# Scale and shift of six feature tiles summed in PSUM by TensorE, with blocks of ada_w as weights

## The chip, the cores and the metric

The kernel runs on one core of a Trainium2 chip. The core has five engines that each take their own instructions in the order in which the program gives them: TensorE (PE; its weight loads are shown apart as PEld), VectorE (DVE), ScalarE (ACT), GpSimd (POOL) and SyncE (SP), whose queue issues most of the DMAs. The metric is the device time of one execution in microseconds. Three executions of the kernel before took 1699.92, 1700.15 and 1702.2 us.

## The reference, cut to what matters

One layer of a decoder trunk: a token-mixing part with four mixers, then an MLP, on 1024 tokens of 1024 features. The part in question is its first step: a normalised input, scaled and shifted per feature, which is then multiplied by the input projection.

```python
c_act = jax.nn.silu(c.astype(jnp.float32))                  # (1, 1024)
mod = (c_act @ ada_w[l] + ada_b[l])[:, None, :]             # (1, 1, 6144)
sh1, sc1, gt1, sh2, sc2, gt2 = jnp.split(mod, 6, axis=-1)
h = rms_norm(x, norm_mix_g[l]) * (1.0 + sc1) + sh1
p = h @ w_in[l]
```

`sh1` and `sc1` are the products of the 1024 values of `c_act` with the first 2048 columns of `ada_w`, which are 8 MB of float32. Every feature of h needs its own sum over 1024 rows of `ada_w`.

## The kernel before, in words

Features lie on partitions, tokens along the free axis. The 1024 features are eight tiles of 128 (`kt`, 0 to 7), the tokens two halves of 512. Each projection is done at float32 precision by three float32r matmuls: h is split into `hh` (rounded) and `hl` (the rest), the weights into `whi` and `wlo`, and `mm3` (L112) adds hh·whi, hl·whi and hh·wlo in PSUM. The text calls these 128x512 matmuls the wide ones.

The stage around the change is `start`. It takes the first three blocks of 128 columns of `w_in` (six PSUM banks, `pts`), loops over the feature tiles, and makes h on the way. For one feature tile `kt`:

- `ada_load` brings the columns of `ada_w` that give sh1 and sc1 of the tile (`ada`, two sections of 128 columns, all eight blocks of 128 rows). Tiles 0 and 1 are loaded alone, 2 and 3, 4 and 5, 6 and 7 in pairs, the pairs into two buffers.
- `ada_sum` multiplies these with `cact` on VectorE, one instruction for each of the eight blocks of rows, and sums them in `aacc`. So 128 partial sums stand on the partitions.
- `ada_col` sums over the partitions: a matmul with `aacc` as weights and a column of ones (L142, output 128x1) for each section, and then two small VectorE instructions (L286, L287) write a column of `sh1` and of `s1`.
- `pre(kt, half)` transposes the tile of x on TensorE (`to_h`, L343), and ScalarE scales and shifts it from PSUM twice (L410), to `hh` and to `ev`; `hl` is their difference (L412), on VectorE for the first half of the tokens and the last tile, on GpSimd for the other half.
- `main(kt, half)` does the nine wide matmuls of the tile and half.

Before that, `norms` squares x (eight ScalarE instructions a half, L352), forms the mean (two VectorE instructions on `st`, L353 and L354), takes the power -1/2 on GpSimd (L355), and scales x (L359 on ScalarE, L361 on VectorE).

The order of the instructions on each engine is set when the program is built: a scheduler takes the instructions as written and places each on its engine by its own estimate of when its inputs are ready. On the chip every engine then keeps to that order, and each instruction waits by semaphores for what it reads and for the buffers that it writes. There are two PSUM banks for `pax`, which the transposes and the sums share. An fp32 matmul (L142, L343) shows in the trace as two pairs of a weight load and a matmul; the text calls such a pair a pass. Two passes are one matmul of `ada_col`.

The order of the wide matmuls, transposes and sums is what the text below follows. Its landmark is the transposition of the second group of parameters (L228, 39 columns), which stands on TensorE near the end of `start`, ahead of the last nine wide matmuls, before and after the change.

Of the kernel before, what the change touches and what calls it, by code (L numbers as in the profile page):

```python
# [10 lines left out]
F32 = mybir.dt.float32  # L11
# [29 lines left out]
class Kern:  # L41
# [212 lines left out]


    def ada_load(self, j, n):

        self.n += 1
        w = self.ADA.tile([P, KT, 2, n * P], F32, tag=f"ada{n}", name=f"ada_{self.n}")
        src = self.a["ada_w"][0].rearrange("(k p) f -> p k f", p=P)  # L260
        for k in (slice(0, KT // 2), slice(KT // 2, KT)):
            for sec in range(2):
                c0 = sec * D + j * P
                self.nc.sync.dma_start(w[:, k, sec], src[:, k, c0 : c0 + n * P])
        return w

    def ada_sum(self, w, n, accs):

        v = self.nc.vector
        self.n += 1  # L270
        acc = self.ADA.tile([P, 2, n * P], F32, tag=f"acc{n}", name=f"aacc_{self.n}")
        accs += [acc[:, :, i * P : i * P + P] for i in range(n)]
        for kt in range(KT):
            if kt == 0:
                v.tensor_scalar(acc, w[:, 0], self.cact[:, 0:1], None, op0=ALU.mult)
            else:
                v.scalar_tensor_tensor(acc, w[:, kt], self.cact[:, kt : kt + 1], acc, op0=ALU.mult, op1=ALU.add)
            yield

    def ada_col(self, j, acc):  # L280
        v = self.nc.vector
        pt = self.ps()
        for sec in range(2):
            self.mm(pt[:, sec : sec + 1], acc[:, sec], self.ones)
        c = slice(j, j + 1)
        v.tensor_tensor(self.sh1[:, c], pt[:, 0:1], self.cols("ada_b")[:, c], op=ALU.add)  # L286
        v.scalar_tensor_tensor(self.s1[:, c], pt[:, 1:2], self.b1[:, c], self.cols("nmg")[:, c], op0=ALU.add, op1=ALU.mult)  # L287
# [76 lines left out]
    def start(self):  # L364
# [21 lines left out]
        self.new_h()  # L386
        raws, ws, accs = [], [], []
        sums = []
        ada = lambda j, n: sums.append(self.ada_sum(self.ada_load(j, n), n, accs))
        xs = [self.load_x(0)]  # L390
# [9 lines left out]

        def add(g, n=KT):
            for _ in range(n):
                next(sums[g], None)

        def pre(kt, half):
            pt = self.to_h(kt, xs[half])
            c = slice(half * HALF, half * HALF + HALF)
            f = self.ev()
            for o in (self.hh[kt][:, c], f):
                nc.scalar.activation(o, pt, AF.Identity, bias=self.sh1[:, kt : kt + 1], scale=self.s1[:, kt : kt + 1])  # L410
            eng = v if kt == KT - 1 or half == 0 else nc.gpsimd
            eng.tensor_tensor(self.hl[kt][:, c], f, self.hh[kt][:, c].bitcast(F32), op=ALU.subtract)  # L412

# [8 lines left out]

        add(0)
        n0 = self.norms(xs[0], True)
        with self.tc.issue_after(sig):
            next(n0)
        self.ada_col(0, accs[0])
        pre(0, 0)
        w_split(0)
        add(1)  # L430
        n1 = self.norms(xs[1])
        for kt in range(KT + 1):
            if kt < KT:
                main(kt, 0)
            if kt + 1 < KT:
                self.ada_col(kt + 1, accs[kt + 1])
                pre(kt + 1, 0)
# [7 lines left out]
            if kt in (1, 2):  # L445
                for _ in (n0, n1)[kt - 1]:
                    pass
            if kt == 0:
                add(2)
            elif kt in (1, 2):  # L450
                add(3, KT // 2)
            elif kt in (3, 4):
                if kt == 3:
                    ada(6, 2)
                    w_load(3)
                add(4, KT // 2)

# [1430 lines left out]
```

## Time and profile before

| | us |
|---|---|
| time, median of 3 (lowest to highest) | 1700.15 (1699.92 to 1702.2) |
| the profiled execution's own time | 1698.43 |
| its span | 1696.7 |
| TensorE busy | 1613.8 (95%) |
| VectorE busy | 1004.0 (59%) |
| ScalarE busy | 652.4 (38%) |
| GpSimd busy | 631.0 (37%) |

The span runs from the first to the last instruction of the profiled execution, and 1.7 us lie around it. TensorE is busy nearly throughout; the busy time of one slice says little of whether it runs at its peak, since the matmuls overlap. A row of the timeline gives the start and the length of an instruction, or of several alike that follow each other (x4), then in brackets how long the engine had idled before it and what released it. The granted clock (PEclk) is a share of full speed.

### The profile page before, as it was taken

How to read it: one execution, taken by the hardware profiler on the slowest of the kernel's cores; microseconds unless marked ns; L12 is line 12 of the kernel's file. 1: busy time of each engine (PE TensorE's matmuls, PEld its weight loads, DVE VectorE, ACT ScalarE, POOL GpSimd, SP SyncE). 2: the span in 40 equal slices, each digit the busy share in tenths (PEclk: the TensorE clock that was granted, in tenths of full speed). 3: DMA queues.
4: the chain of work that ended last, by engine and by line, in shares of the span. 5: the costliest groups of instructions: out<-in, count | busy, mean ns of one | idle time of the engine just before them, and what ended most of it. 6: DMA issues, size and time to landing. Idle time of an engine off the chain costs nothing.

```text
span 1696.7 us, 22664 instructions
## 1 busy us (share of the span) xinstructions
PE 1613.8 (95%) x8083; PEld 1293.7 (76%) x8083; DVE 1004.0 (59%) x1729; ACT 652.4 (38%) x1206; POOL 631.0 (37%) x505
## 2 busy tenths in 40 slices
PE   3999999999999999999999998799999999999996
PEld 2798778777777777777888876588888878888875
DVE  5673545666538824233433567865555469669986
ACT  4522124556522112211222245544455446444343
POOL 2260223112220223222101374576556565128662
PEclk9999999999999999999999999799999999999998
DMA  8423136777675345331211446354444485562332
GB/s 276 131 63 66 52 118 195 180 188 175 143 151 182 63 138 174 107 116 35 75 48 62 170 146 172 92 178 150 154 157 141 161 309 170 161 223 87 99 125 99
DMA packets 262723, 234.68 MB, mean 138 GB/s; under 512 B 79351, under 2 KB 194282, under 8 KB 262610
## 3 DMA queue, kind: packets, MB, share of 16 engines
q1 hardware_dynamic: 254002, 224.83, 44.2%
q10 hardware_dynamic: 8464, 8.01, 1.9%
q8 instruction: 64, 1.05, 0.3%
q0 software_dynamic: 144, 0.39, 0.1%
q14 instruction: 49, 0.40, 0.1%
HBM read 172.59 MB, written 60.58 MB: 137 GB/s over the span
## 4 chain that ended last, share of the span: by engine, by line
PE 37%; DVE 8%; DMA 2%; issue 2%; ACT 2%; POOL 1%; POOLq 0%; DVEq 0%; ACTq 0%; SPq 0%
PE pmm L112 22%; PE pax L112 8%; PE pch L112 7%; DVE g L73 2%; DVE xx L73 1%; DMA raw<-in_ffn_w_dram 1%; DVE m L1523 1%; DMA raw<-FA 1%; DMA w<-in_ffn_w_dram 1%; ACT g L72 1%; DVE wlo L73 0%; POOL ev L1513 0%; DVE m L1526 0%; DVE m L1328 0%; DVE n L73 0%
## 5 line engine op out<-in xcount | busy, mean ns | idle before, releaser
L112 PE MATMUL pmm<-hh,whi 128*128 128x512 f32 x704 | 285.3, 407 | 3.9 <-ACT hh L410 3.9
L112 PE MATMUL pmm<-hl,whi 128*128 128x512 f32 x704 | 278.7, 396 | 5.3 <-POOL hl L412 4.1
L112 PE MATMUL pmm<-hh,wlo 128*128 128x512 f32 x704 | 278.3, 395 | 0.0
L73 DVE TENSOR_TENSOR wlo<-raw,whi 128x512 fp32r<-128x512 f32 (+1 forms) x140 | 105.8, 793 | 129.4 <-ACT whi L72 126.1
L112 PEld LDWEIGHTS pmm<-hh,whi 128*128 128x128 f32 x704 | 132.6, 189 | 34.7 <-ACT hh L410 5.1
L112 PEld LDWEIGHTS pmm<-hl,whi 128*128 128x128 f32 x704 | 133.2, 189 | 33.6 <-POOL hl L412 4.5
L112 PEld LDWEIGHTS pmm<-hh,wlo 128*128 128x128 f32 x704 | 133.2, 189 | 29.7 <-issue 0.9
L72 ACT CAST whi<-raw 128x512 fp32r<-128x512 f32 (+1 forms) x140 | 79.0, 612 | 158.2 <-PE pmm L112 141.5
L112 PE MATMUL pmm<-g,g 128*128 128x512 f32 x456 | 107.3, 390 | 0.6 <-DVE xx L1425 0.6
L112 PE MATMUL pmm<-n,wyh 128*128 128x512 f32 x320 | 106.3, 411 | 0.8 <-ACT n L72 0.8
L73 DVE TENSOR_TENSOR g<-raw,g 128x512 fp32r<-128x512 f32 x75 | 72.0, 959 | 48.7 <-ACT g L72 42.6
L112 PEld LDWEIGHTS pmm<-g,g 128*128 128x128 f32 x456 | 85.6, 188 | 18.9 <-DVE xx L1425 1.0
L1239 POOL TENSOR_TENSOR m<-m,sig 128x512 f32<-128x512 f32 x32 | 45.1, 1409 | 129.9 <-DVE sig L1236 129.8
L1222 ACT ACTIVATE sig<-pmm 128x512 f32<-128x512 f32 x64 | 38.1, 596 | 142.6 <-PE pmm L112 131.4
L84 POOL TENSOR_TENSOR raw<-raw,gt 128x1024 f32<-128x1024 f32 x16 | 39.1, 2444 | 136.3 <-DMA raw<-in_w_o_dram 131.6
L112 PE MATMUL pmm<-g,m 128*128 128x512 f32 x256 | 82.5, 404 | 3.4 <-ACT m L72 3.4
L1236 DVE TENSOR_TENSOR sig<-pmm,sig 128x512 f32<-128x512 f32 x48 | 32.9, 686 | 69.0 <-PE pmm L112 68.9
L72 ACT CAST g<-raw 128x512 fp32r<-128x512 f32 x75 | 46.5, 620 | 69.8 <-PE pmm L112 34.6
L112 PEld LDWEIGHTS pmm<-n,wyh 128*128 128x128 f32 x320 | 60.5, 193 | 16.4 <-issue 1.2
L73 DVE TENSOR_TENSOR n<-xx,m 128x512 fp32r<-128x512 f32 x64 | 54.9, 863 | 28.4 <-ACT m L72 28.3
L72 ACT CAST m<-xx 128x512 fp32r<-128x512 f32 x64 | 39.3, 620 | 75.8 <-PE pch L112 27.4
L112 PE MATMUL pch<-g,g 128*128 128x512 f32 x222 | 59.7, 402 | 8.7 <-DVE g L73 5.7
(480 smaller groups left out, 3833.3 us busy)
## 6 DMA issues: line engine op xcount, KB each, us to landing
raw<-FA SPq DMA_DIRECT2D x56, 512.0 KB
raw<-in_w_in_dram SPq DMA_DIRECT2D x52, 512.0 KB
FA<-xx SPq DMA_DIRECT2D x80, 256.0 KB
raw<-in_ffn_w_dram SPq DMA_DIRECT2D x36, 512.0 KB
mod<-in_ada_w_dram SPq DMA_DIRECT2D x64, 256.0 KB
w<-in_ffn_w_dram SPq DMA_DIRECT2D x32, 512.0 KB
raw<-in_w_o_dram SPq DMA_DIRECT2D x16, 512.0 KB
FA<-ev SPq DMA_DIRECT2D x32, 256.0 KB
```

What stands on the lines that cost most here:

```text
L72: a = nc.scalar.copy(hi, src)
L73: b = (eng or nc.vector).tensor_tensor(lo, src, hi.bitcast(F32), op=ALU.subtract)
L84: nc.gpsimd.tensor_tensor(raw, raw, scale, op=ALU.mult)
L112: mm = lambda *x, **y: self.nc.tensor.matmul(*x, **y, skip_group_check=open_)
L1222: nc.scalar.activation(sg, pg, AF.Sigmoid)
L1236: v.tensor_tensor(m if first else sg, py[0], sg, op=ALU.mult)
L1239: nc.gpsimd.tensor_tensor(m, m, sg, op=ALU.add)
L1523: v.tensor_tensor(dst, x, y, op=ALU.add)
```

## The change

For the tiles 0 to 5 `ada_sum` goes. `ada_col` now sums over all 1024 rows in PSUM: sixteen matmuls for a tile (eight blocks of rows, two sections), each with a 128x128 block of `ada_w` as weights and a column of `cact` as the moving operand. The tiles 6 and 7 keep the sum on VectorE (`summed`). The calls are placed anew in the loop: tile 1 after the wide matmuls of tile 0, tiles 2 and 3 after those of tile 1, tiles 4 and 5 after those of tile 3, tiles 6 and 7 after those of tile 5; the load of 6 and 7 moves from kt 3 to kt 1. All `hl` are made on VectorE, those of the second half too. Lines of the kernel after are three higher from `norms` on (L286 is L289, L353 is L356).

```diff
--- before.py
+++ after.py
...
@@ -264,24 +265,26 @@
                 self.nc.sync.dma_start(w[:, k, sec], src[:, k, c0 : c0 + n * P])
         return w
 
-    def ada_sum(self, w, n, accs):
+    def ada_sum(self, w, n):
 
         v = self.nc.vector
         self.n += 1
-        acc = self.ADA.tile([P, 2, n * P], F32, tag=f"acc{n}", name=f"aacc_{self.n}")
-        accs += [acc[:, :, i * P : i * P + P] for i in range(n)]
-        for kt in range(KT):
-            if kt == 0:
-                v.tensor_scalar(acc, w[:, 0], self.cact[:, 0:1], None, op0=ALU.mult)
-            else:
-                v.scalar_tensor_tensor(acc, w[:, kt], self.cact[:, kt : kt + 1], acc, op0=ALU.mult, op1=ALU.add)
-            yield
-
-    def ada_col(self, j, acc):
+        acc = self.ADA.tile([P, 2, n * P], F32, tag="acc", name=f"aacc_{self.n}", bufs=1)
+        v.tensor_scalar(acc, w[:, 0], self.cact[:, 0:1], None, op0=ALU.mult)
+        for kt in range(1, KT):
+            v.scalar_tensor_tensor(acc, w[:, kt], self.cact[:, kt : kt + 1], acc, op0=ALU.mult, op1=ALU.add)
+        return acc
+
+    def ada_col(self, j, w, i, summed=False):
         v = self.nc.vector
         pt = self.ps()
+        f = slice(i * P, i * P + P)
         for sec in range(2):
-            self.mm(pt[:, sec : sec + 1], acc[:, sec], self.ones)
+            if summed:
+                self.mm(pt[:, sec : sec + 1], w[:, sec, f], self.ones)
+                continue
+            for kt in range(KT):
+                self.mm(pt[:, sec : sec + 1], w[:, kt, sec, f], self.cact[:, kt : kt + 1], kt == 0, kt == KT - 1)
         c = slice(j, j + 1)
         v.tensor_tensor(self.sh1[:, c], pt[:, 0:1], self.cols("ada_b")[:, c], op=ALU.add)
         v.scalar_tensor_tensor(self.s1[:, c], pt[:, 1:2], self.b1[:, c], self.cols("nmg")[:, c], op0=ALU.add, op1=ALU.mult)
@@ -384,9 +387,14 @@
         self.b1 = self.ADA.tile([P, 8], F32, tag="b1", name="b1", bufs=1)
         v.tensor_scalar(self.b1, self.cols("ada_b")[:, 8:16], 1.0, None, op0=ALU.add)
         self.new_h()
-        raws, ws, accs = [], [], []
-        sums = []
-        ada = lambda j, n: sums.append(self.ada_sum(self.ada_load(j, n), n, accs))
+        raws, ws = [], []
+        adas = {}
+
+        def ada(j, n):
+            w = self.ada_load(j, n)
+            for i in range(n):
+                adas[j + i] = w, i
+
         xs = [self.load_x(0)]
         ada(0, 1)
         w_load(0)
@@ -398,18 +406,13 @@
         w_load(2)
         pts = [self.ps(t) for t in ("mm", "mm", "mm", "mm", "ch", "ch")]
 
-        def add(g, n=KT):
-            for _ in range(n):
-                next(sums[g], None)
-
         def pre(kt, half):
             pt = self.to_h(kt, xs[half])
             c = slice(half * HALF, half * HALF + HALF)
             f = self.ev()
             for o in (self.hh[kt][:, c], f):
                 nc.scalar.activation(o, pt, AF.Identity, bias=self.sh1[:, kt : kt + 1], scale=self.s1[:, kt : kt + 1])
-            eng = v if kt == KT - 1 or half == 0 else nc.gpsimd
-            eng.tensor_tensor(self.hl[kt][:, c], f, self.hh[kt][:, c].bitcast(F32), op=ALU.subtract)
+            v.tensor_tensor(self.hl[kt][:, c], f, self.hh[kt][:, c].bitcast(F32), op=ALU.subtract)
 
         def main(kt, half):
             hi, lo = (z[:, kt % 2] for z in ws[kt // 2])
@@ -420,20 +423,26 @@
                 if kt == KT - 1:
                     self.pa_out(b, half, pts[2 * b + half])
 
-        add(0)
         n0 = self.norms(xs[0], True)
         with self.tc.issue_after(sig):
             next(n0)
-        self.ada_col(0, accs[0])
+        self.ada_col(0, *adas[0])
         pre(0, 0)
         w_split(0)
-        add(1)
         n1 = self.norms(xs[1])
         for kt in range(KT + 1):
             if kt < KT:
                 main(kt, 0)
+            for j in {0: (1,), 1: (2, 3), 3: (4, 5), 5: (6, 7)}.get(kt, ()):
+                self.ada_col(j, *adas[j], summed=j > 5)
+            if kt == 1:
+                ada(6, 2)
+                w_load(3)
+            elif kt == 3:
+                acc = self.ada_sum(adas[6][0], 2)
+                for j in (6, 7):
+                    adas[j] = acc, j - 6
             if kt + 1 < KT:
-                self.ada_col(kt + 1, accs[kt + 1])
                 pre(kt + 1, 0)
                 w_split(kt + 1)
             if kt == 0:
@@ -445,15 +454,6 @@
             if kt in (1, 2):
                 for _ in (n0, n1)[kt - 1]:
                     pass
-            if kt == 0:
-                add(2)
-            elif kt in (1, 2):
-                add(3, KT // 2)
-            elif kt in (3, 4):
-                if kt == 3:
-                    ada(6, 2)
-                    w_load(3)
-                add(4, KT // 2)
 
     def pa_out(self, b, hf, pt):
         e = self.ev()

```

The order on VectorE at the program's start, before. `aacc` is the sum of tile 0, `st` the squares' mean, `m` a tile of x, `sh` and `s` the shift and scale:

```order
L250 TENSOR_TENSOR cact<-cact,prmT 128x8
L275 TENSOR_SCALAR aacc_204<-ada_156,cact 128x256
L277 SCALAR_TENSOR_TENSOR aacc_204<-ada_156,cact,aacc_204 128x256 x4
L353 TENSOR_TENSOR st_33_213<-st_33_213 128x4
L277 SCALAR_TENSOR_TENSOR aacc_204<-ada_156,cact,aacc_204 128x256
L354 TENSOR_SCALAR st_33_213<-st_33_213 128x4
L277 SCALAR_TENSOR_TENSOR aacc_204<-ada_156,cact,aacc_204 128x256
L361 TENSOR_SCALAR m_141<-m_141,st_33_213 128x512
L277 SCALAR_TENSOR_TENSOR aacc_204<-ada_156,cact,aacc_204 128x256
L73 TENSOR_TENSOR wlo_252<-raw_161,whi_251 128x384
L286 TENSOR_TENSOR sh_95<-pax_237,prmT 128x1
L287 SCALAR_TENSOR_TENSOR s_94<-pax_237,b_122,prmT 128x1
```

And after the change:

```order
L250 TENSOR_TENSOR cact<-cact,prmT 128x8
L289 TENSOR_TENSOR sh_95<-pax_228,prmT 128x1
L290 SCALAR_TENSOR_TENSOR s_94<-pax_228,b_122,prmT 128x1
L356 TENSOR_TENSOR st_32_204<-st_32_204 128x4
L357 TENSOR_SCALAR st_32_204<-st_32_204 128x4
L364 TENSOR_SCALAR m_141<-m_141,st_32_204 128x512
L364 TENSOR_SCALAR m_145<-m_145,st_32_204 128x512
L364 TENSOR_SCALAR m_149<-m_149,st_32_204 128x512
L364 TENSOR_SCALAR m_153<-m_153,st_32_204 128x512
```

The two instructions on `st` stood between the steps of the sum and ahead of `sh` and `s`; now they stand behind `sh` and `s` of tile 0, which read the PSUM sum of all sixteen matmuls (`pax_228`).

The order on ScalarE where the second half of x is squared (L352, after the change L355), before. `hh_2_125` and `ev_283` are feature tile 1 of the first half, `hh_2_124` is tile 0 of the second half; four more squares stand directly above these rows:

```order
L352 ACTIVATE n_298,st_49_289<-m_176 128x512
L352 ACTIVATE n_300,st_49_289<-m_177 128x512
L410 ACTIVATE hh_2_125<-pax_278,sh_95,s_94 128x512
L410 ACTIVATE ev_283<-pax_278,sh_95,s_94 128x512
L352 ACTIVATE n_302,st_49_289<-m_180 128x512
L352 ACTIVATE n_304,st_49_289<-m_181 128x512
L410 ACTIVATE hh_2_124<-pax_313,sh_95,s_94 128x512
```

And after the change, where no square stands above these rows:

```order
L355 ACTIVATE n_300,st_47_299<-m_168 128x512
L414 ACTIVATE hh_2_125<-pax_288,sh_95,s_94 128x512
L414 ACTIVATE ev_293<-pax_288,sh_95,s_94 128x512
L355 ACTIVATE n_302,st_47_299<-m_169 128x512
L355 ACTIVATE n_304,st_47_299<-m_172 128x512
L355 ACTIVATE n_306,st_47_299<-m_173 128x512
L355 ACTIVATE n_308,st_47_299<-m_176 128x512
L355 ACTIVATE n_310,st_47_299<-m_177 128x512
L355 ACTIVATE n_312,st_47_299<-m_180 128x512
L355 ACTIVATE n_314,st_47_299<-m_181 128x512
L414 ACTIVATE hh_2_124<-pax_323,sh_95,s_94 128x512
```

Six of the eight squares stood ahead of tile 1's `hh`; now one does, and seven stand behind its `ev`.

The order on TensorE from the third wide matmul on tile 0's second half to the first transposition for tile 2, before (`pmm_199`, `pmm_201` and `pch_203` are the banks of the second half, `pax_340` the sum of tile 2):

```order
L112 MATMUL pch_203<-hh_2_124,whi_251 128x512
L112 MATMUL pmm_199<-hl_2_132,whi_251 128x512
L112 MATMUL pmm_199<-hh_2_124,wlo_252 128x512
L112 MATMUL pmm_201<-hl_2_132,whi_251 128x512
L112 MATMUL pmm_201<-hh_2_124,wlo_252 128x512
L112 MATMUL pch_203<-hl_2_132,whi_251 128x512
L112 MATMUL pch_203<-hh_2_124,wlo_252 128x512
L142 MATMUL pax_340<-ones,aacc_322 128x1 x2
L343 MATMUL pax_345<-ident,m_140 128x128
```

And after the change (`pax_341` and `pax_360` are the sums of tiles 2 and 3):

```order
L112 MATMUL pch_203<-hh_2_124,whi_256 128x512
L142 MATMUL pax_341<-cact,ada_184 128x1 x8
L142 MATMUL pax_360<-cact,ada_184 128x1 x12
L112 MATMUL pmm_199<-hl_2_132,whi_256 128x512
L112 MATMUL pmm_199<-hh_2_124,wlo_257 128x512
L112 MATMUL pmm_201<-hl_2_132,whi_256 128x512
L112 MATMUL pmm_201<-hh_2_124,wlo_257 128x512
L142 MATMUL pax_341<-cact,ada_184 128x1 x4
L142 MATMUL pax_360<-cact,ada_184 128x1 x4
L112 MATMUL pch_203<-hl_2_132,whi_256 128x512
L112 MATMUL pch_203<-hh_2_124,wlo_257 128x512
L346 MATMUL pax_386<-ident,m_140 128x128
```

Between these wide matmuls and the transposes of tile 2 there stood two matmuls for a sum; now 28 stand there, among the wide ones, and four more stand a few rows earlier, among the transposes of the second half.

## Rows read from the trace of the kernel before

**Rows 1.** The page: the span.

```profile
span 1696.7 us, 22664 instructions
```

**Rows 2.** Busy time by stretches, all engines. Columns: stretch (us from the span's start) and its length, then busy us and number of instructions of PE, PEld, DVE, ACT and POOL, then granted clock, DMA share, GB/s.

```profile
20.00:30.00 10.00, 7.84 (x25) 5.20 (x25) 6.34 (x18) 7.93 (x20) 0.00 (x0) 1.00 1.07 364
30.00:40.00 10.00, 4.04 (x14) 2.09 (x13) 8.31 (x18) 3.23 (x8) 4.89 (x2) 0.90 0.87 283
40.00:50.00 10.00, 8.76 (x38) 6.99 (x38) 9.03 (x14) 2.79 (x4) 1.68 (x2) 0.76 0.61 201
50.00:60.00 10.00, 8.85 (x46) 6.84 (x46) 9.37 (x18) 6.39 (x10) 1.57 (x2) 1.00 0.35 106
...
100.00:120.00 20.00, 20.00 (x85) 20.00 (x85) 17.91 (x40) 2.67 (x6) 15.65 (x12) 1.00 0.19 54
```

**Rows 3.** Timeline of the program's start, to the first wide matmuls.

```profile
12.37 0.19 ACT L352 ACTIVATION_READ_ACCUMULATOR n<-m 128x1 f32 x1
13.76 0.35 DVE L275 TENSOR_SCALAR aacc<-ada,cact 128x256 f32<-128x256 f32 x1 [9.50 <-DMA ada<-in_ada_w_dram]
14.14 2.05 DVE L277 SCALAR_TENSOR_TENSOR aacc<-ada,cact,aacc 128x256 f32<-128x256 f32 x4
16.11 0.15 DVE L353 TENSOR_TENSOR st<-st 128x4 f32<-128x4 f32 x1
...
18.15 2.56 ACT L359 ACTIVATE m<-m,st 128x512 f32<-128x512 f32 x4 [1.14 <-POOL st L355]
19.09 1.01 PE L142 MATMUL pax<-ones,aacc 128*128 128x1 f32 x4 [15.59 <-DVE aacc L277]
...
20.22 0.21 DVE L287 SCALAR_TENSOR_TENSOR s<-pax,b,prmT 128x1 f32<-128x1 f32 x1
...
21.28 0.78 ACT L410 ACTIVATE hh<-pax,sh,s 128x512 fp32r<-128x512 f32 x1 [0.17 <-PE pax L343]
...
21.96 0.77 ACT L410 ACTIVATE ev<-pax,sh,s 128x512 f32<-128x512 f32 x1
...
22.11 1.22 PE L112 MATMUL pmm<-hh,whi 128*128 128x512 f32 x2 [0.87 <-ACT hh L410]
```

**Rows 4.** Timeline of TensorE alone: two neighbouring passes of 128x1 in the sum of tile 1; then the second and the eighth weight load of a run of eight such passes in a later stage (sums of `mods`, on `macc`).

```profile
26.98 0.35 PE L142 MATMUL pax<-ones,aacc 128*128 128x1 f32 x1
27.20 0.35 PE L142 MATMUL pax<-ones,aacc 128*128 128x1 f32 x1
...
314.75 0.19 PEld L142 LDWEIGHTS pax<-ones,macc 128*128 128x128 f32 x1
...
315.42 0.19 PEld L142 LDWEIGHTS pax<-ones,macc 128*128 128x128 f32 x1
```

**Rows 5.** Timeline of TensorE: neighbouring wide matmuls early and later.

```profile
25.21 0.63 PE L112 MATMUL pmm<-hl,whi 128*128 128x512 f32 x1
...
25.64 0.63 PE L112 MATMUL pmm<-hh,wlo 128*128 128x512 f32 x1
...
64.49 0.39 PE L112 MATMUL pmm<-hh,whi 128*128 128x512 f32 x1
...
64.72 0.39 PE L112 MATMUL pmm<-hl,whi 128*128 128x512 f32 x1
```

**Rows 6.** Timeline from the last squares of the second half of x to the first wide matmuls of tile 2.

```profile
29.65 0.62 ACT L352 ACTIVATE n<-m 128x512 f32<-128x512 f32 x1
...
30.26 0.62 ACT L352 ACTIVATE n<-m 128x512 f32<-128x512 f32 x1
...
31.01 0.16 DVE L353 TENSOR_TENSOR st<-st 128x4 f32<-128x4 f32 x1 [0.53 <-ACT n L352]
...
32.50 1.67 DVE L361 TENSOR_SCALAR m<-m,st 128x512 f32<-128x512 f32 x4 [1.13 <-POOL st L355]
...
33.04 1.52 PE L343 MATMUL pax<-ident,m 128*128 128x128 f32 x4 [0.85 <-DVE m L361]
...
35.43 0.73 PE L112 MATMUL pmm<-hh,whi 128*128 128x512 f32 x2 [0.87 <-ACT hh L410]
...
36.12 4.27 POOL L412 TENSOR_TENSOR hl<-ev,hh 128x512 fp32r<-128x512 f32 x1 [3.66 <-ACT ev L410]
...
40.45 0.79 PE L112 MATMUL pmm<-hl,whi 128*128 128x512 f32 x1 [4.05 <-POOL hl L412]
...
43.88 1.48 PE L343 MATMUL pax<-ident,m 128*128 128x128 f32 x8
...
45.78 0.73 PE L112 MATMUL pmm<-hh,whi 128*128 128x512 f32 x2 [0.43 <-ACT hh L410]
```

**Rows 7.** Busy time and granted clock by stretches (columns as in rows 2).

```profile
40.00:44.00 4.00, 3.55 (x11) 2.85 (x12) 3.22 (x5) 0.00 (x0) 0.39 (x1) 0.50 0.02 3
44.00:45.00 1.00, 1.00 (x8) 1.00 (x8) 0.94 (x3) 0.05 (x1) 0.00 (x0) 0.64 0.77 212
...
437.40:440.80 3.40, 1.93 (x18) 1.63 (x17) 1.92 (x4) 1.87 (x2) 0.00 (x0) 0.98 0.65 176
440.80:444.20 3.40, 3.40 (x9) 2.70 (x10) 1.68 (x3) 0.00 (x0) 0.00 (x0) 0.52 0.85 248
```

**Rows 8.** Timeline of TensorE at the landmark.

```profile
80.59 0.25 PE L228 MATMUL pax<-ident,prm 39*128 39x39 f32 x1
```

**Rows 9.** Instructions on the tile `aacc`: engine, number, duration in ns (least, median, most), first and last start, forms.

```profile
L277 DVE SCALAR_TENSOR_TENSOR aacc<-ada,cact,aacc x35: 477/740/1830, 14.1 to 60.0; 128x512 f32<-128x512 f32 x21, 128x256 f32<-128x256 f32 x14
```

## The prediction

> **What bounds the kernel now.** I read the span first [rows 1], then busy time by stretches [rows 2]. Later than the stage `start` TensorE is full: 20.00 us busy in the 20 us from 100, with 85 matmuls, and VectorE's 17.91 us lie beside them. Time lost or won in `start` therefore goes on to the end. In `start` TensorE is not full: 4.04 us busy between 30 and 40 us, 8.76 and 8.85 in the next two stretches, while VectorE has 8.31 to 9.37. So I went to the timelines. At the very start TensorE waits for VectorE's sum of tile 0 and then for x: the first wide matmul begins at 22.11 [rows 3]. Then it waits for the second half of x, whose first transposition is at 33.04, and from 36.4 to 40.45, 4.05 us, for the `hl` that GpSimd makes in 4.27 us [rows 6]. Tile 2 begins at 45.78, the landmark comes at 80.59 [rows 8].
>
> The granted clock matters here. [...] At the low level wide matmuls follow each other at 0.43 us, at the full one at 0.23 [rows 5]. Those that begin at 22.11 run at 0.43 too, though the column reads 1.00 there [rows 2]; I take the spacing as the evidence. A pass of 128x1 takes 0.215 us (27.20 less 26.98) at the low level; at the full one the second to eighth weight loads of a run lie 0.67 us apart in six steps, 0.112 us each [rows 4].
>
> **What goes, and what it is worth.** Of the five sums four leave VectorE, 28 of 35 of the multiply-add steps at 0.48 to 0.74 us [rows 9], some 19 us with their first steps. None of it is on the path by itself once the passes stand in its place: what ends these waits is a sum per tile, whoever makes it. The GpSimd `hl` of 4.27 us goes, with its wait of 4.05 us and the low clock after it; I follow below what is late there next. The seven `hl` now on VectorE fit in the room that the sums leave. DMA volume and order stay as they were, so all data lands when it did.
>
> **What comes, step by step.** A tile takes 16 matmuls, 32 passes: 3.6 us at full clock, 6.9 at the low one. No row shows so long a run of such passes, and none says which clock it gets; these two are the bounds. I take the low price until a run of wide matmuls has lasted 4.3 to 5 us, because it was so both times that the clock rose in this stage, and because the engine also lost the clock while busy: in the 3.40 us from 437.4 it was busy for 1.93 us with short matmuls, and the next stretch was granted 0.52 [rows 7].
>
> *First wide matmul.* The loads of tile 0 let VectorE begin at 13.76, and its fifth step, on the second halves, followed without a gap [rows 3]. TensorE needs one load of the four to begin, so I let it begin at 13.5: 32 passes at 0.215 end at 20.4. VectorE's `sh` and `s` end 0.33 later (20.43 after 20.10 in rows 3), at 20.75. Now comes the turn that the order makes: `st` of x stands behind them on VectorE. It began at 16.11 and would begin at 20.75, though the squares end at 12.56 as before. From `st` to the scaling of x takes 1.49 us (31.01 to 32.50 in rows 6), so 22.2 in place of 18.15. From there to ScalarE's `hh` took 3.1 us [rows 3]: the transposes end at 25.3. Eight of tile 1's 32 passes lie in the waits between the transposes, 24 stand ahead of the first wide matmul: 5.2 us more. It begins at 30.5, not 22.11.
>
> [...]
>
> *Second half of x.* From 30.5 TensorE has 18 wide matmuls and four transposes, which I take at 0.215 each like the passes: at the low clock up to about 35.5 ten of them are done, the others take 1.9 us, end 37.4. On ScalarE tile 1's transposes end at 32.65, its `hh` and `ev` take 0.68 each [rows 3], and seven squares stand behind them at 0.61 (29.65 to 30.26): the last begins at 37.7, not 30.26, and the chain to the first transposition shifts by as much, from 33.04 to 40.5. So the wait for GpSimd is replaced by one of 3.1 us for the squares.
>
> *Tiles 2 and 3.* From the first transposition to the first wide matmul took 2.4 us [rows 6]; eight passes among them add 0.6: 43.5. Three wide at the low clock (1.3), 40 passes (8.6), four wide (1.7), 16 passes (3.4), two wide (0.9): 59.4. From the transposes to the first wide matmul of tile 2 took 1.9 us (43.88 to 45.78): 61.3 in place of 45.78, a loss of 15.5 us.
>
> *From there to the landmark.* Wide matmuls and transposes are as many as before. The clock rises some 4.3 us after 59.4, so 2.4 us run at half: 1.2 us lost. In place of 20 passes for five tiles there are 64 for tiles 4 and 5 and 8 for tiles 6 and 7: 52 more at 0.112 are 5.8 us. The 64 stand in one run; I let the clock fall after 5 us of it, so the last 20 cost 0.103 more each, 2.1 us, and the wide ones after it 2.4 us. Together 10.3. The 2.4 us for which TensorE idles between 40 and 60 us in rows 2 may shrink or not; I leave them.
>
> Sum: 15.5 + 1.2 + 10.3 = 27.0 us. The profiled execution took 1698.43 us, 1.7 around its span of 1696.7; it becomes 1725.4. It lies 1.7 under the median of 1700.15, so I say 1727. The steps carry some 7 us either way, mostly from when the clock rises and falls: 1720 to 1734.
>
> **Rivals.** *The passes get the full clock.* Then only the start is low: 20 passes up to 17.8, 12 at 0.112, `s` at 19.45, scaling at 20.9, transposes to 24.0, 24 passes of 2.7 us, first wide matmul at 26.7. 18 wide and the transposes end at 31.3; squares end so that the second half's first transposition is at 35.7; 2.4 + 2.1 + 6.3 + 1.9 us later tile 2 begins, at 48.4, 2.6 us late. With 5.8 us to the landmark that is 8.4, and 2.1 more if the 4.4 us wait at 31.3 drops the clock as the one before 40.45 did: about 9.5, so 1709 to 1711. For it: TensorE is then hardly ever without an instruction. Against it: in a pass only one column moves, and the trace has short matmuls ahead of a fall. [...]
>
> *TensorE takes the passes in its idle time, and it comes out no slower.* Besides tile 0 and 24 passes of tile 1 the change adds 116 passes: 13.0 us. Between 30 and 60 us 8.4 us of idle time could go [rows 2], and the two spells at the low clock cost about 2.3 each: 13.0 against 13.0, 1700. This is decided where `st` begins: only if tile 0's sum is there by about 16 us does the first wide matmul stay at 22.11. The loads end too late for that: 32 passes even at 0.112 need 3.6 us, and the last eight of them can't begin before the fourth load has landed, near 15.5.
>
> *The clock stays low longer,* through the wide matmuls between the runs of passes, which waits keep breaking: each further 10 us at 0.50 costs 5, so 1735 and above.
>
> **How the numbers follow.** My forecast 0.63, the full clock 0.20, between these two 0.05, low for longer 0.07, no slower 0.05 (of which 0.02 faster). 0.2% is 3.4 us, about what a measurement of this kernel can tell from no change. All but the last case are slower by more than that. The range reaches from the full-clock case to the end of my own, 1706 to 1735; for the likeliest alone it is 1720 to 1734.
>
> **What would show it.** First wide matmul near 30 us (26.7: the full-clock case; 22: no loss); VectorE's first `st` behind `sh`, near 21 us; the second half's first transposition near 40 us with seven squares just ahead; granted clock 0.50 in or just behind the run of 64 passes; the landmark near 107 us, and the same distance from it to the end. If passes of the long runs lie 0.11 us apart, my price is wrong; if the landmark is late but the end is not, the stages behind it took the loss up.

## The result and the profile after

The changed kernel took 1721.03 us (median of 4 runs, 1720.43 to 1722.23), the kernel before 1701.18 beside it (4 runs, 1699.92 to 1702.94): ratio 1.0123, 95% interval 1.011 to 1.0137. It is slower by 19.9 us. The profiled execution took 1722.23, 23.8 more than that of before; of the gap between 19.9 and 23.8 most is that the profiled execution of before (1698.43) lay 2.8 under its median here. What follows compares the two traces. Where experiments ran on other chips, their ratios are compared, not their microseconds.

From the page of the changed kernel, the span and the two engines that changed:

```profile
span 1720.5 us, 22969 instructions
...
PE 1650.5 (96%) x8251; PEld 1333.6 (78%) x8251; DVE 987.3 (57%) x1704; ACT 652.3 (38%) x1206; POOL 620.2 (36%) x498
```

The timeline of the changed kernel, from the passes of tile 0 to the landmark (against [rows 3, 6, 8]; lines from `norms` on stand three to four higher than before, L343 is L346, L361 is L364). First TensorE, then VectorE in the start, then the last square on ScalarE:

```profile
12.22 6.99 PE L142 MATMUL pax<-cact,ada 128*128 128x1 f32 x32 [8.70 <-DMA ada<-in_ada_w_dram]
...
29.21 1.20 PE L112 MATMUL pmm<-hh,whi 128*128 128x512 f32 x2
...
32.77 0.63 PE L112 MATMUL pmm<-hh,wlo 128*128 128x512 f32 x1
33.20 0.63 PE L112 MATMUL pch<-hl,whi 128*128 128x512 f32 x1
...
35.34 0.39 PE L112 MATMUL pmm<-hh,wlo 128*128 128x512 f32 x1
35.57 0.39 PE L112 MATMUL pch<-hl,whi 128*128 128x512 f32 x1
...
39.63 0.30 PE L346 MATMUL pax<-ident,m 128*128 128x128 f32 x1 [3.45 <-DVE m L364]
39.77 1.01 PE L142 MATMUL pax<-cact,ada 128*128 128x1 f32 x8
...
43.82 8.53 PE L142 MATMUL pax<-cact,ada 128*128 128x1 f32 x40
...
54.06 3.41 PE L142 MATMUL pax<-cact,ada 128*128 128x1 f32 x16
...
60.25 1.13 PE L112 MATMUL pmm<-hh,whi 128*128 128x512 f32 x2
...
67.85 10.42 PE L142 MATMUL pax<-cact,ada 128*128 128x1 f32 x64
78.13 0.77 PE L112 MATMUL pmm<-hh,whi 128*128 128x512 f32 x1
...
103.48 0.25 PE L228 MATMUL pax<-ident,prm 39*128 39x39 f32 x1
...
19.24 0.16 DVE L289 TENSOR_TENSOR sh<-pax,prmT 128x1 f32<-128x1 f32 x1 [14.95 <-PE pax L142]
19.32 0.21 DVE L290 SCALAR_TENSOR_TENSOR s<-pax,b,prmT 128x1 f32<-128x1 f32 x1
19.44 0.15 DVE L356 TENSOR_TENSOR st<-st 128x4 f32<-128x4 f32 x1
...
37.50 0.16 DVE L356 TENSOR_TENSOR st<-st 128x4 f32<-128x4 f32 x1 [3.59 <-ACT n L355]
...
36.75 0.62 ACT L355 ACTIVATE n<-m 128x512 f32<-128x512 f32 x1
```

The landmark comes at 103.48, 22.9 us later than the 80.59 of [rows 8]; from there to the end of the span it is 1617.0 us, and 1616.1 before. So nearly the whole loss lies in the first hundred microseconds. From the landmark to the end it is 1613.8 to 1618.0 us in the profiles of the runs below; a difference at the landmark that is smaller than these 4 us can't be told at the end of one profile. Most of the 22.9 us, 14.5, is there when tile 2 begins (60.25 against 45.78 in [rows 6]); the other 8.4 come between tile 2 and the landmark. A reader sees the price of the passes in the runs: 40 in 8.53 us is 0.213 each, 16 in 3.41 the same, the 32 of tile 0 in 6.99 is 0.218. The wide matmuls that follow the start lie 0.43 us apart (32.77 and 33.20), 0.23 from about 33.6 on (35.34 and 35.57), as in [rows 5].

Busy time and granted clock in stretches of the changed kernel (columns as in rows 2; the last row is from tile 2 to the landmark):

```profile
40.00:50.00 10.00, 9.13 (x43) 8.44 (x43) 2.96 (x7) 1.85 (x3) 0.00 (x0) 0.53 0.07 15
50.00:60.00 10.00, 10.00 (x41) 9.14 (x41) 1.03 (x5) 0.58 (x1) 0.00 (x0) 0.50 0.13 39
60.00:70.00 10.00, 9.98 (x58) 8.46 (x56) 4.26 (x7) 6.32 (x11) 0.00 (x0) 0.94 0.68 214
70.00:80.00 10.00, 10.00 (x53) 9.70 (x53) 1.74 (x6) 0.00 (x0) 1.09 (x2) 0.57 0.24 70
...
60.25:103.48 43.23, 43.23 (x225) 37.53 (x225) 19.73 (x42) 22.36 (x36) 1.80 (x3) 0.87 0.34 100
```

The same stretch of the kernel before:

```profile
45.78:80.59 34.81, 33.29 (x172) 26.34 (x173) 23.05 (x41) 20.86 (x33) 9.62 (x9) 1.00 0.40 121
```

Against [rows 2] TensorE has lost its idle time (8.76 and 8.85 in the ten microseconds from 40 and from 50 have become 9.13 and 10.00), and with it the clock: 0.53 and 0.50 where it had been 0.76 and 1.00. From 70 to 80 it is busy for 10.00 of 10.00 us and granted 0.57. A full column of busy time is here the sign of a slow engine, not of a well used one.

### The profile page after: what moved, and what is told of

Same layout as the page of the kernel before. It is cut to its first block, busy times and chain, and to the rows that moved or that the text cites. A ratio compares the mean times of both kernels' runs of the same rounds, so it can differ in the third digit from the quotient of the medians.

```text
span 1720.5 us, 22969 instructions
## 1 busy us (share of the span) xinstructions
PE 1650.5 (96%) x8251; PEld 1333.6 (78%) x8251; DVE 987.3 (57%) x1704; ACT 652.3 (38%) x1206; POOL 620.2 (36%) x498
## 4 chain that ended last, share of the span: by engine, by line
PE 36%; DVE 8%; issue 3%; DMA 2%; ACT 2%; POOL 1%; POOLq 0%; DVEq 0%; ACTq 0%; SPq 0%
PE pmm L112 21%; PE pax L112 7%; PE pch L112 7%; DVE g L73 2%; DVE xx L73 1%; DVE m L1523 1%; DMA raw<-FA 1%; DMA w<-in_ffn_w_dram 1%; DMA raw<-in_ffn_w_dram 0%; DVE xx L1425 0%; ACT g L72 0%; DVE n L73 0%; POOL ev L1513 0%; DVE m L1526 0%; DVE m L1328 0%
## 5 line engine op out<-in xcount | busy, mean ns | idle before, releaser
L112 PEld LDWEIGHTS pmm<-n,wyh 128*128 128x128 f32 x320 | 61.1, 195 | 16.3 <-issue 1.2
```

The source lines that it names most:

```text
L112: mm = lambda *x, **y: self.nc.tensor.matmul(*x, **y, skip_group_check=open_)
```

## The experiments

The theory: TensorE runs the passes of one column at the low clock, or falls to it during them, and this is what the change costs. The rivals: the wait of `st` in the start costs it; `hl` moved to VectorE does; the mere number of passes does; the new order of the start does.

**The start: `st` ahead of `sh` and `s`.** Nothing else of the changed kernel moves but what follows from it.

```diff
-        v.tensor_scalar(st[:, 2], st[:, 2], 1.0 / D, 1e-6, op0=ALU.mult, op1=ALU.add)
+        self.mean = v.tensor_scalar(st[:, 2], st[:, 2], 1.0 / D, 1e-6, op0=ALU.mult, op1=ALU.add).ins
...
-        self.ada_col(0, *adas[0])
+        with self.tc.issue_after(self.mean):
+            self.ada_col(0, *adas[0])
```

> The change, but VectorE takes the two instructions on st of the first half of x ahead of sh and s of tile 0; nothing else moves. Order theory (st held behind tile 0's sum delays the first wide matmul): st begins near 12.5 us, not 19.44; TensorE is then the last thing waited for, and 32 + 8 + 24 passes at 0.215 and four transposes from 12.2 put the first wide matmul at about 27.0, not 29.2; everything behind it shifts by about as much, 1719 us. Rival (the passes alone set the start, the order of st costs nothing): first wide matmul stays at 29.2, 1721 us.

Measured: 1722.15 us, ratio 1.0133 (1.0119 to 1.0147), no gain. The first wide matmul came at 27.22, the 2 us earlier that the step says, and the second half's first transposition at 37.63 in place of 39.63. TensorE's timeline shows where the 2 us went from there:

```profile
37.63 0.45 PE L346 MATMUL pax<-ident,m 128*128 128x128 f32 x1 [4.02 <-DVE m L364]
37.87 1.73 PE L142 MATMUL pax<-cact,ada 128*128 128x1 f32 x8
...
42.65 8.53 PE L142 MATMUL pax<-cact,ada 128*128 128x1 f32 x40
...
102.83 0.25 PE L228 MATMUL pax<-ident,prm 39*128 39x39 f32 x1
```

Behind the wait for the second half of x (now 4.02 us, not 3.45) the passes already have the price of the low clock: the eight take 1.73 us (0.216 each), not 1.01, and the 40 passes begin only 1.2 us earlier (42.65 against 43.82). At the landmark 0.65 us is left, less than the end can show. The start step is sized right, and is not what the time hangs on.

**`hl` on GpSimd again, in the changed kernel; and on VectorE in the kernel before.** First the one:

```diff
-            v.tensor_tensor(self.hl[kt][:, c], f, self.hh[kt][:, c].bitcast(F32), op=ALU.subtract)
+            eng = v if kt == KT - 1 or half == 0 else nc.gpsimd
+            eng.tensor_tensor(self.hl[kt][:, c], f, self.hh[kt][:, c].bitcast(F32), op=ALU.subtract)
```

> The change, but hl of the second half of the tokens (tiles 0 to 6) back on GpSimd. If GpSimd's 4.27 us were its own, the wait for the first of them would return: up to 4 us slower, 1725 us. My theory: it was slow because VectorE summed beside it; without the sums it takes about 1.3 us, and the 40 passes in front of its reader hide it: within 1 us of the change, 1721 us.

The other is the same edit turned round, in the kernel before:

```diff
-            eng = v if kt == KT - 1 or half == 0 else nc.gpsimd
-            eng.tensor_tensor(self.hl[kt][:, c], f, self.hh[kt][:, c].bitcast(F32), op=ALU.subtract)
+            v.tensor_tensor(self.hl[kt][:, c], f, self.hh[kt][:, c].bitcast(F32), op=ALU.subtract)
```

> The kernel before with one part of the change alone: all hl on VectorE, the sums as before. If the wait of 4.05 us for GpSimd and the fall of the clock behind it were worth something, TensorE resumes near 38 us instead of 40.45 and keeps or sooner regains the full clock: 2 to 5 us faster than before, about 1697 us. Rival: VectorE is full there (8.31 to 9.37 of 10 us) and hl queues behind the sums: no change, 1701 us.

Measured: the first 1721.66, ratio 1.0136 (1.012 to 1.0151): nothing to be told from the change as it stands. TensorE waited for none of the seven `hl`, as expected; in the kernel before GpSimd took 4.27 for the first alone, 1.29 to 1.37 for the other six. Two of these six began while VectorE summed (47.82 and 53.59) and took 1.29, so the sums beside it, by themselves, are not shown to be the reason for the 4.27; that stays open. (In its profile the landmark came at 106.03, 2.6 us later, but the end 0.7 us earlier. The passes began 1.0 us late there, and the eight behind a wait of 4.04 us took 1.73.) The second 1694.09, ratio 0.9975 (0.9965 to 0.9986), and on another chip 1695.26, ratio 0.9988 (0.9978 to 0.9998). So this part alone gains some 2 to 4 us on the kernel before, and the sums in PSUM cost more than the total shows. TensorE in the kernel before with `hl` on VectorE:

```profile
36.57 0.50 PE L112 MATMUL pmm<-hl,whi 128*128 128x512 f32 x1 [0.44 <-DVE hl L411]
...
42.76 0.98 PE L142 MATMUL pax<-ones,aacc 128*128 128x1 f32 x4 [3.62 <-DVE aacc L277]
```

The wait of 4.05 us for GpSimd [rows 6] is gone, and 3.62 us of waiting for VectorE's sum of tile 2 stand behind it: most of what the one gave, the other took.

**The run of 64 passes, with 128 equal columns moved.** The weights, their number and the place of the passes stay; `cact` is broadcast, so that each pass moves 128 columns of the same values, of which one is read (the second section's result moves to column 128 with it). This is done for tiles 4 and 5 alone.

```diff
+        m = P if j in (4, 5) else 1
...
-                self.mm(pt[:, sec : sec + 1], w[:, kt, sec, f], self.cact[:, kt : kt + 1], kt == 0, kt == KT - 1)
+                self.mm(pt[:, sec * P : sec * P + m], w[:, kt, sec, f], self.cact[:, kt : kt + 1].to_broadcast([P, m]), kt == 0, kt == KT - 1)
```

> The change, but the matmuls of tiles 4 and 5 move 128 columns (cact's column repeated) in place of one, the same weights and the same number of passes; columns past the first are not read. Clock theory (runs of one-column passes lose the full clock): the run of 64 passes takes 7.2 to 8.2 us, not 10.3, the granted clock stays 1.00 through it, and the wide matmuls behind it follow at 0.23 us: 2 to 4 us faster than the change, about 1718 us. Rival (the passes are slow for their weights, whatever moves): 10.3 us again or longer, 1721 us or more.

Measured: 1715.06, ratio 1.0094 (1.008 to 1.0108). Its timeline of TensorE, and its windows:

```profile
67.91 7.31 PE L142 MATMUL pax<-cact,ada 128*128 128x128 f32 x64
...
98.63 0.25 PE L228 MATMUL pax<-ident,prm 39*128 39x39 f32 x1
```

```profile
70.00:80.00 10.00, 10.00 (x73) 9.23 (x72) 5.52 (x11) 2.79 (x4) 1.09 (x2) 1.00 0.36 93
```

The same 64 passes take 3.1 us less while they move 128 times as many columns, the clock stays at 1.00 where it was 0.57, and the landmark comes 4.85 us earlier. TensorE's busy column reads 10.00 in both, so that column can't tell them apart.

**Tiles 4 and 5 summed on VectorE again,** tiles 0 to 3 left in PSUM (`aacc` gets a second buffer):

```diff
-                self.ada_col(j, *adas[j], summed=j > 5)
+                self.ada_col(j, *adas[j], summed=j > 3)
...
                 w_load(3)
+                acc = self.ada_sum(adas[4][0], 2)
+                for j in (4, 5):
+                    adas[j] = acc, j - 4
```

> After, with the sum of tiles 4 and 5 back on VectorE, so that the run of 64 passes becomes 4 matmuls of one column; tiles 0 to 3 stay in PSUM. The forecast's third part (the run of 64 and the low clock behind it): until the wide matmuls of tile 2 nothing changes (60 us), then the landmark comes 10 to 13 us earlier, at 91 to 93.5 (103.48 less 10.3 for the run, less up to 2.5 for the low clock behind it, 0.9 back for the four matmuls), and the time is 1708 to 1711. Rival (VectorE becomes late with this sum, as before the change it was with tile 2's): TensorE waits at the four matmuls for aacc, the landmark comes at 97 or later, 1714 or more.

Measured: 1713.34, ratio 1.0084 (1.0071 to 1.0097): against the change's 1.0123 a gain of 6.6 us, where 10 to 13 were expected. TensorE's timeline:

```profile
61.45 1.22 PE L112 MATMUL pmm<-hh,whi 128*128 128x512 f32 x2
...
72.64 1.02 PE L142 MATMUL pax<-ones,aacc 128*128 128x1 f32 x8 [0.77 <-DVE aacc L275]
...
96.28 0.25 PE L228 MATMUL pax<-ident,prm 39*128 39x39 f32 x1
```

From tile 2 to the landmark it is 34.83 us, what it was before the change (34.81), against 43.23: the run of 64 with all that hangs on it is worth 8.4 us, of which the experiment before gives 4.85 to the clock. Most of what was missed is in the start, which ran 1.2 us later in this profile (61.45 against 60.25), and in idle time: TensorE is busy for 33.64 of these 34.83 us, where the passes had filled all of 43.23. Of these 1.2 us of idle time 0.77 are a wait for `aacc`, as the rival said.

**128 equal columns for all six tiles:** the edit of tiles 4 and 5 without its `m`. With it the scheduler also changes the order of the start: `st` comes ahead of `sh` and `s`, and five of the eight squares ahead of tile 1's `hh`.

```diff
-                self.mm(pt[:, sec : sec + 1], w[:, kt, sec, f], self.cact[:, kt : kt + 1], kt == 0, kt == KT - 1)
+                self.mm(pt[:, sec * P : sec * P + P], w[:, kt, sec, f], self.cact[:, kt : kt + 1].to_broadcast([P, P]), kt == 0, kt == KT - 1)
```

> After, with 128 equal columns moved in place of one in the matmuls of all six tiles (same weights, same passes, the same result in every column; with it the scheduler puts st ahead of sh and s). Theory (passes of one column lose the full clock, and that is most of the loss): the 40 and 16 passes of tiles 2 to 5 take 4.6 and 1.8 us in place of 8.53 and 3.41, the run of 64 takes 7.2 to 7.4 as with the last two tiles alone, the wide matmuls of tile 2 begin between 48 and 54 us in place of 60.25, the landmark comes at 88 to 93 (98.6 with the last two tiles alone), the time is 1705 to 1710 us. Rival (the order of the work in the start costs it, not the clock): the wide matmuls of tile 2 begin at 57 or later, the landmark at 96 or later, 1713 or more.

Measured: 1697.5, ratio 0.9993 (0.9984 to 1.0002): the loss is gone. Of the expectation the sign came true and the sizes did not: 1705 to 1710 was too cautious, and so were tile 2 at 48 to 54 (it begins at 42.58) and the landmark at 88 to 93. Timeline of TensorE and windows:

```profile
12.31 5.79 PE L142 MATMUL pax<-cact,ada 128*128 128x128 f32 x32 [8.64 <-DVE st L356]
...
20.74 0.72 PE L112 MATMUL pmm<-hh,whi 128*128 128x512 f32 x2
...
33.37 6.41 PE L142 MATMUL pax<-cact,ada 128*128 128x128 f32 x56
...
42.58 0.40 PE L112 MATMUL pmm<-hh,whi 128*128 128x512 f32 x1
...
49.65 7.31 PE L142 MATMUL pax<-cact,ada 128*128 128x128 f32 x64
...
80.52 0.25 PE L228 MATMUL pax<-ident,prm 39*128 39x39 f32 x1
```

```profile
40.00:50.00 10.00, 9.97 (x54) 8.25 (x52) 4.70 (x9) 6.38 (x10) 0.00 (x0) 1.00 0.78 254
50.00:60.00 10.00, 9.97 (x81) 9.40 (x80) 5.49 (x12) 2.57 (x4) 1.09 (x2) 1.00 0.33 88
```

56 passes take 6.41 us, 0.114 each, where 40 and 16 took 8.53 and 3.41. The granted clock is 1.00 in every ten microseconds from 30 to 80. The gain begins at the very start: the first 32 passes take 5.79 us in place of 6.99, and the first wide matmul comes at 20.74, not 29.21. Tile 2 begins 3.2 us earlier than in the kernel before (45.78), the 64 passes take that back, and the landmark stands where it stood before the change, 80.52 against 80.59, with all the added passes.

**The order of the start alone.** Since the last kernel moved two things, this one moves only the order, with one column: `st` first as above, and the squares of the second half called ahead of tile 1's part (two of the eight then come before its `hh`, six before its `ev`).

```diff
+            if kt == 0:
+                next(n1)
             if kt + 1 < KT:
                 pre(kt + 1, 0)
                 w_split(kt + 1)
-            if kt == 0:
-                next(n1)
```

> After with one column moved, but the start in nearly the order that the kernel with 128 columns everywhere got: st ahead of sh and s of tile 0, and most of the seven squares of the second half of x ahead of tile 1's hh and ev. Theory (what gained 23 us there was the clock, not the order): a pass still takes 0.215 in the start, the 40 and 16 passes 8.5 and 3.4 us, the granted clock is 0.50 behind a wait as before; the second half's first transposition comes earlier, at 31 to 36, and up to 3 us may be kept of it: landmark at 98 to 103, 1717 to 1722. Rival (the order of the start made the gain): tile 2 begins at 52 or earlier, the landmark at 95 or earlier, 1712 or less.

Measured: 1716.97, ratio 1.0112 (1.0094 to 1.0131), within the interval of the change itself; the landmark at 99.66. TensorE and the windows:

```profile
34.63 0.39 PE L112 MATMUL pmm<-hh,wlo 128*128 128x512 f32 x1
34.87 0.40 PE L112 MATMUL pmm<-hl,whi 128*128 128x512 f32 x1
...
36.92 0.30 PE L346 MATMUL pax<-ident,m 128*128 128x128 f32 x1 [0.96 <-DVE m L364]
37.06 1.01 PE L142 MATMUL pax<-cact,ada 128*128 128x1 f32 x8
...
39.33 0.72 PE L112 MATMUL pmm<-hh,whi 128*128 128x512 f32 x2 [0.87 <-ACT hh L414]
...
40.12 8.52 PE L142 MATMUL pax<-cact,ada 128*128 128x1 f32 x40
...
64.03 10.55 PE L142 MATMUL pax<-cact,ada 128*128 128x1 f32 x64
```

```profile
40.00:50.00 10.00, 10.00 (x46) 9.67 (x45) 0.67 (x1) 0.34 (x1) 0.00 (x0) 0.51 0.00 0
```

The order brings the landmark 3.8 us forward; at the end nothing of it can be told. The 40 passes still cost 0.213 each, and tile 2 begins at 56.54, where the rival had 52 or earlier. Between this kernel and the last the order is not quite the same, so the split is not exact; but some four fifths of the 23 us at the landmark stay for the 128 columns and the clock that they keep. The other half of this comparison, 128 columns with the order of the changed kernel, was not run.

**Versions meant to be faster.** Tile 0 alone in PSUM with 128 columns, `st` first, all `hl` on VectorE, the rest of the kernel before:

```diff
+            if j == 0:
+                for kt in range(KT):
+                    self.mm(pt[:, sec * P : sec * P + P], acc[:, kt, sec], self.cact[:, kt : kt + 1].to_broadcast([P, P]), kt == 0, kt == KT - 1)
+                continue
```

> Before, with all hl on VectorE (1694.09 by itself), and tile 0 alone in PSUM, 128 equal columns moved, st placed ahead of its sh and s; tiles 1 to 7 are summed on VectorE as before. Theory (what the change could win is at the first wide matmul, and only while the passes keep the full clock and st does not wait): 32 passes from 12.2 end at 16.5 to 19.2, the first wide matmul begins at 18.5 to 21.2 in place of 22.11, tile 1's sum is ready earlier too; the landmark comes at 74 to 78 (78.3 with hl alone), 1690 to 1694 us. Rival (the start is bound by the second half of x and its squares, or by the sum of tile 2): the first wide matmul is earlier, but the wide matmuls of tile 2 begin at 45 us as before, and the time stays at 1694 within 1 us.

Measured: 1699.15, 12 runs from 1693.0 to 1701.44, ratio 1.0002 (0.9992 to 1.0011): no gain. The profile is of the shortest, 1693.0. It shows the first wide matmul at 20.22 (22.36 with `hl` alone), and then this:

```profile
41.44 0.58 PE L142 MATMUL pax<-ones,aacc 128*128 128x1 f32 x4 [3.27 <-DVE aacc L277]
```

TensorE waits here for the sum of tile 2 as it does with `hl` alone (3.62 us there), and the gain of the start is kept in this profile: tile 2 begins at 43.60 (45.57 with `hl` alone), the landmark comes at 76.46 (78.28), as the theory has it. But ten of the twelve runs took 1698.1 us or more, outside the range of the theory and of the rival alike. The mean granted clock of those ten is 0.979 to 0.982, that of the two shortest 0.985; where they lose it this trace can't show, and why stays open.

Then 128 columns for tiles 0 to 3, and tiles 4 and 5 summed on VectorE (the edits of the six tiles and of the sum on VectorE together):

```diff
+                self.mm(pt[:, sec * P : sec * P + P], w[:, kt, sec, f], self.cact[:, kt : kt + 1].to_broadcast([P, P]), kt == 0, kt == KT - 1)
...
+                self.ada_col(j, *adas[j], summed=j > 3)
...
+                acc = self.ada_sum(adas[4][0], 2)
```

> After, with 128 equal columns moved for tiles 0 to 3, and tiles 4 and 5 summed on VectorE again, with 4 matmuls of one column for them. Theory (a pass with 128 columns keeps the clock and costs only its 0.114 us; the passes of tiles 0 to 3 fill time in which TensorE had waited, those of tiles 4 and 5 stand on the full engine): until tile 2 nothing changes against 128 columns everywhere, then the run of 64 (7.31 us) becomes 4 matmuls of about 0.5 to 1 us, the landmark comes at 73.5 to 75 (80.52), 1689.5 to 1692 us. Rival (VectorE ends the sum of tiles 4 and 5 late, TensorE waits for aacc and the clock falls with it): 2 to 4 us idle at those matmuls, the landmark at 77 or later, 1693 or more.

It ran beside the kernel before with `hl` on VectorE.

> Before with all hl on VectorE, once more on the same chip as the mixed kernel, to compare the two: 1692 to 1696 us as the first time; the mixed kernel is to be 2 to 5 us faster by the theory, no faster by its rival.

Measured: 1691.03 (5 runs, 1690.38 to 1692.6), ratio 0.9955 (0.9942 to 0.9969): faster than the kernel before by 7.5 us and than the one beside it (1695.26) by 4.2. TensorE and a window:

```profile
33.28 6.41 PE L142 MATMUL pax<-cact,ada 128*128 128x128 f32 x56
...
49.30 0.95 PE L142 MATMUL pax<-ones,aacc 128*128 128x1 f32 x8
...
74.03 0.25 PE L228 MATMUL pax<-ident,prm 39*128 39x39 f32 x1
```

```profile
40.00:50.00 10.00, 10.00 (x57) 8.39 (x55) 9.15 (x16) 6.38 (x10) 0.00 (x0) 1.00 0.77 253
```

No wait stands ahead of the eight passes on `aacc`, VectorE is busy for 9.15 of the 10 us, and the landmark comes 6.5 us earlier than with all six tiles in PSUM. By the ratio that `hl` alone had on the other chip (0.9975) the gain over it is 3.4 us rather than 4.2; all five runs lie below the fastest of the kernel beside it (1693.54). The time and the landmark are as the theory has them (1689.5 to 1692, 73.5 to 75). So for tiles 0 to 3 together the change's idea is sound; its form, one column at a time, was not. Which of these four tiles pay, no run separates.

## Why the prediction was right

The sign, the mechanism and its place were right: slower, by the passes at the low clock, nearly all of it ahead of the landmark. The time, 1721.03, lies in the likeliest case's range (1720 to 1734), but at its lower end, 6 us under the 1727 named. Between the two profiles the loss is 23.8 us, where the sum gave 27.0; between the medians it is 19.9, because the profiled execution before lay 2.8 under its median.

- **Price of a pass.** 0.215 us was taken; the long runs show 0.213 to 0.218. At the full clock the forecast had 0.112 from [rows 4], and the passes of 128 columns took 0.114 there; the long runs of one column, at the low clock, took about twice that.
- **First wide matmul.** Forecast 30.5, measured 29.21. The passes began at 12.22, not 13.5: the load that TensorE waits for landed earlier than I had taken from VectorE's start. The steps behind that are as forecast, 1.1 to 1.3 us earlier. The turn of `st` behind `sh` is in the rows (19.24, 19.32, 19.44).
- **Second half of x.** First transposition forecast 40.5, measured 39.63, with the wait of 3.45 us for the squares in place of the 3.1 named. The clock rose about 4.4 us after the first wide matmul, by the spacing of the wide matmuls (0.43 us up to 33.62, 0.23 from 34.65 on); the column reads 1.00 there throughout.
- **Tiles 2 and 3.** Tile 2 forecast 61.3, measured 60.25; a loss of 14.5 us against 15.5. The runs of 40 and 16 passes took 8.53 and 3.41 against 8.6 and 3.4.
- **From there to the landmark.** Forecast 11.5 (the 1.2 of the clock and the 10.3), measured 8.4. This is the term that was mis-sized. The 1.5 us for which TensorE idled in this stretch (33.29 busy of 34.81) went, which the forecast left out. The clock rose at about 61.2 (granted 0.50 to 61.1, 1.00 from 61.2), 2.9 us after the transposes began at 58.32, where the forecast took the 4.3 us of [rows 6, 7] (40.45 to about 44.7); that costs 0.5 in place of 1.2. Behind the run it was low for 3.5 us (78.13 to 81.6, granted 1.00 from 81.7), 1.8 in place of 2.4. Against these the run itself took 10.28 us, where the forecast's terms give 9.2: the clock fell at about 71.4 (granted 1.00 from 70 to 71, 0.69 from 71 to 72, 0.50 from 72 to 73), 3.5 us into the run and not 5; the 5 was the author's estimate, and no run shows it. About 1.3 us of the difference is not traced to one row. The landmark came at 103.5, not 107.
- **The rivals.** *The passes get the full clock* did not happen. The kernel with 128 columns makes it happen and takes 1697.5, not the 1709 to 1711 of this rival. That is no test of its price as it stands, since the order of the start changed too: the rival kept `st` behind the sum and let tile 2 begin 2.6 us late, where it began 3.2 us early. From tile 2 to the landmark it had 5.8 us for the passes, where 3.1 were added (37.94 against 34.81): it left the idle time of TensorE alone, which the passes fill (busy 37.91 of 37.94). That is in effect the third case, in which TensorE takes the passes in its idle time. That kernel has the full clock and `st` ahead of the sum, and the changed kernel neither; `st` ahead alone was not enough (102.83 at the landmark), the full clock without it was not tried. *The clock stays low longer* did not come: it was back within a few microseconds of wide matmuls each time, at about 61.2 and 81.6.
- **What goes.** The forecast followed the GpSimd `hl` only to what is late next. The runs show its worth: 2 to 4 us on the kernel before, nothing that can be told in the changed one, where the squares are late instead. The forecast also said that the order of the DMAs stays, but the load of tiles 6 and 7 moved forward; TensorE does not wait ahead of their eight passes at 89.92, so this changed nothing in the sum.

## What to carry to other kernels

Before work is moved to TensorE as matmuls of one column, look at the granted clock beside the busy time: such a run stood at half the clock here (0.50 from 44 to 52) or fell to it (0.57 from 70 to 80) while the profile called the engine fully busy, and the wide matmuls behind it paid as well (granted 0.50 from 78.1 to 81.6). Broadcasting the moving column to 128 costs next to no time (0.114 us a pass at the full clock, against 0.112 with one column) and here, with the order of the start that came with it, bought back the whole loss. And split a change by parts: of this one, the `hl` on VectorE was a gain by itself, and the sums were worth moving for tiles 0 to 3 and not for 4 and 5.

## What the runs showed of the hardware that was not expected

- The clock fell in the middle of a run during which TensorE never waited: 64 passes of one column from 67.85, granted 0.57 in the stretch 70 to 80; the fall lies at about 71.4. With the same weights and 128 columns it stayed at 1.00.
- Moving 128 times as many columns took less time, not more: 7.31 us against 10.42 for the same 64 passes.
- The 32 passes at the very start took 6.99 us with one column moved, 0.218 each to the end; with 128 columns for all six tiles they took 5.79 (6.70 in the kernel with tile 0 alone), and there the wide matmuls behind them lay 0.23 us apart at once (22.69 and 22.92), not 0.43.
- In the order experiment the 40 passes from 40.12 took 8.52 us although the eight at 37.06 had run in 1.01, the full clock's price. Wide matmuls had lain 0.23 us apart just before (34.63 and 34.87), two waits of under 1 us lie between, and the stretch 40 to 50 is granted 0.51: the clock was lost no later than within the first of the passes. The 4.05 us wait of the kernel before is thus not needed for the fall. (The column's 1.00 from 30 to 40 says little there, since it also stands beside wide matmuls 0.43 us apart, 30.24 and 30.67.)
